# Interleaving the columns of two weight blocks in a float32 decoder layer, so that the matmuls read with a step of two

## The chip, the cores and the metric

The kernel runs on one core of one Trainium2 chip. The metric is the device time of one execution in microseconds (us), less being better. The core's engines are TensorE (PE: matmuls; PEld: the loads of its stationary operand), VectorE (DVE), ScalarE (ACT), GpSimd (POOL) and SyncE (SP), which here issues most of the DMAs. All matmul operands lie in SBUF, the on-chip memory of 128 partitions; matmuls accumulate into PSUM banks of 128 x 512 float32.

## The reference

One decoder layer on 256 tokens of width 2048, in float32. An input projection feeds two token mixers (16-head latent attention and a short causal convolution), each gated with SiLU. What concerns the change is the end, in which five matrices of 2048 x 2048 are applied to 256 tokens:

```python
g_mla, g_conv = h @ w_in[..., -4096:-2048], h @ w_in[..., -2048:]
y_mla  = einsum('bse,ed->bsd', attn, w_o_mla)
y_conv = einsum('bse,ed->bsd', b_gate * conv * silu(z_conv), w_o_conv)
merged = sigmoid(g_mla) * y_mla + sigmoid(g_conv) * y_conv
out    = einsum('bsd,de->bse', merged, w_out)
x      = x + _rmsnorm(out, post_norm_g)
```

(The first line is shortened: the two gates are the last 4,096 columns of the projection of the normalised input `h`.)

## The kernel before

*Precision.* Every float32 matrix product is made of three matmuls on rounded parts (type float32r): a value is split into `hi` (rounded by ACT, L245) and `lo` (the rest, by DVE, L246), and `product` issues `hi*hi`, `hi*lo` and `lo*hi` into the same PSUM bank (L88 is the line of all matmuls). The stationary operand is a block of 128 x 128 of the activations (128 features, 128 tokens), the moving operand a block of 128 x 512 of the weights: 128 input features in the partitions, 512 output columns in a row. One matmul gives 128 tokens by 512 output columns.

*Weights.* All weights come through one list of units, `plan`, in the order of use. A unit is 128 x 2048 float32 (1,024 KB), that is four blocks of 128 x 512, for four neighbouring groups of 128 input features (k4 = 0 to 3) of one quarter of the output columns. `load_raw` brings a unit into one of three `raw` buffers (L161, SP's queue), `split_unit` splits each half of it (`HALF` = 1,024 columns, so two blocks) into a tile `whi` and a tile `wlo` of 128 x 1024, and `take` returns `piece(j, n)`, which cuts the j-th block of n columns out of the half in which it lies: block 0 and 1 out of the first pair of tiles, 2 and 3 out of the second.

*Merged stage* (matmuls named `sq`). Over four quarters c of the output columns, over the four matrices n (two gates from `x_both`, the attention's output product from `at_both`, the convolution's from `cv_both`), over four units kk, over two token tiles t and the four blocks k4 of the unit: a `product` each. That is 4 x 4 x 4 x 2 x 4 x 3 = 1,536 matmuls. Its units are `u_d[c][n][kk]`.

*Output product* (matmuls named `out`). Over four column quarters and four units, two token tiles and four blocks, from `m_both`: 4 x 4 x 2 x 4 x 3 = 384 matmuls; its units are `u_out[c, kk]`, which come last in the plan. Each stage's units come out of the array `wsq` (five matrices), which the host lays out before the launch; the device time has no part of that. In the ending the second token tile's result is finished with three small plain-float32 matmul pairs (`fin`).

*Order.* Matmuls stand in the order in which they are written; a scheduler places the rest around them, and SP's loads wait until a `raw` buffer is free. Stages ahead of the merged one read units of other arrays (`cv` and `z` matmuls among them, which have the same shape of 128 x 512).

Of the kernel before, what the change touches and what calls it, by code (L numbers as in the profile page):

```python
# [18 lines left out]
P = 128  # L19
# [18 lines left out]
UNIT = 2048  # L38
LINE = 32
HALF = UNIT // 2  # L40
# [42 lines left out]
def tile_layer(ctx: ExitStack, tc: tile.TileContext, xw, w0, xb, x, pos, pvec, post_g, wc, wz, wcv, wkr, wqk, wqr, wv, cwr, wsq, out):  # L83
# [22 lines left out]
    def add(ap, width=UNIT):  # L106
        plan.append((ap, width))
        return len(plan) - 1
# [30 lines left out]
    u_d = [[[add(wsq[n, c, k]) for k in range(4)] for n in range(4)] for c in range(4)]  # L139
# [62 lines left out]
    def ahead(i, raw=3, split=1):  # L202
        while done["raw"] < min(i + raw, len(plan)):
            load_raw(done["raw"])
            done["raw"] += 1
        while done["split"] < min(i + 1 + split, len(plan)):
            while done["raw"] <= done["split"]:
                load_raw(done["raw"])
                done["raw"] += 1
            split_unit(done["split"])  # L210
            done["split"] += 1

    def take(i):
        ahead(i)
        parts = splits.pop(i)

        def piece(j, n):
            o = j * n
            h, o = o // HALF, o % HALF
            return parts[h][0][:, o : o + n], parts[h][1][:, o : o + n]  # L220

        return piece
# [81 lines left out]
    n = 2 * XW // S  # L304
# [202 lines left out]
    for i in range(KD // 2):  # L507
# [3 lines left out]
        w = take(u_qa[i])  # L511
# [3 lines left out]
    for i in range(4):  # L515
        w = take(u_ckv[i])
# [9 lines left out]
    w = splits.pop(u_kr)  # L526
# [150 lines left out]
    def values(h, pt):  # L677
        vv = groups["v", h // HV]
        j = h % HV
        o = bank(f"o{h}", tag="o", bufs=1)  # L680
        vs = slice(j * DV, (j + 1) * DV)
        both = o[:, :].rearrange("p (i q) -> p i q", i=2)
        mm = matmul
        mm(both, vv[0][:, 0, vs], pt[:, :, :S], start=True, stop=False)
        yield
        mm(o[:, :S], vv[1][:, 0, vs], pt[:, 0, :S], start=False, stop=False)
        mm(o[:, P:S], vv[1][:, 1, vs], pt[:, 0, S:], start=False, stop=False)
        mm(both[:, :, P:], vv[0][:, 1, vs], pt[:, :, S:], start=False, stop=True)

        at = at_t[:, h // HV, :, :].rearrange("p t (i k x) -> p t i k x", i=4, k=HV)[:, :, :, j, :]  # L690
        f = temp("f")
        whole(f[:, :], o)
        nc.vector.tensor_tensor(at, f[:, :].rearrange("p (t i x) -> p t i x", t=NT, i=4), at, op=ALU.mult)
# [119 lines left out]
    for h in range(H):  # L813
        v, at = divmod(h, HV)

        if at == 0:
            for i in range(4):
# [13 lines left out]
                elif v and i == 2:  # L831
                    o = values(h - 1, pt)
# [171 lines left out]
    for i, (c, kk) in enumerate(out_order[:3]):  # L1004
        w = take(u_out[c, kk])
# [188 lines left out]
```

## Time and profile before

| What | Value |
|---|---|
| Median of 2 runs | 1035.01 us (1034.82 and 1035.21) |
| Span of the profiled execution, first to last instruction | 1033.7 us |
| Merged stage (`sq`), from 590.5 to 938.7 us | 348.2 us, 1,536 matmuls |
| Output product (`out`), from 938.7 to 1025.7 us | 87.0 us, 384 matmuls |
| Ending after the last `out` matmul | 8 us |
| Mean granted TensorE clock | 1.000 |
| HBM traffic | 221 GB/s over the span |

The profile is of one execution. The only time of its own that it has is its span; the two timed runs lie 1.1 and 1.5 us above it. A matmul's duration in it (389 ns for 512 columns) is longer than the distance from one matmul's start to the next, since they overlap in the array; the pace is read from the starts, or from a piece's length over its count. `out<-in` names the tile that an instruction writes and those that it reads. An arrow behind an idle time names what ended it.

### The profile page before, as it was taken

What the parts mean: (1) busy time and instruction counts of PE and PEld (TensorE: products, weight loads), DVE (VectorE), ACT (ScalarE), POOL (GpSimd) and SP (SyncE); (2) the same over time, 40 slices, a digit from 0 to 9 for tenths busy, and PEclk for the clock granted to TensorE, in tenths of its full rate; (3) what the DMA queues carried; (4) which work ended last, traced back from release to release, by engine and by line L of the source; (5) the groups of instructions that cost most, each with busy time, mean ns of one, the idle gap of its engine ahead of it and who ended that gap; (6) DMA issues with size and microseconds to landing.
All of it is one profiled execution on the core that took longest, in us unless ns stands there. A gap on an engine that the chain in (4) does not pass through costs nothing.

```text
span 1033.7 us, 12740 instructions
## 1 busy us (share of the span) xinstructions
PE 1027.6 (99%) x4684; PEld 856.7 (83%) x4684; DVE 683.5 (66%) x957; ACT 527.4 (51%) x735; POOL 178.7 (17%) x344
## 2 busy tenths in 40 slices
PE   9999999999999999999999999999999999999998
PEld 8888888888888888888888888888888888888886
DVE  7588787787777777777777785564455455455562
ACT  7665545655456454564555565344434444443451
POOL 4540421104300223112133120020010001002000
PEclk9999999999999999999999999999999999999999
DMA  9775865668665676857686765565565557558642
GB/s 353 278 261 204 276 221 219 211 197 288 215 250 193 223 265 209 275 187 242 228 270 226 265 217 199 204 226 185 200 219 209 188 201 241 183 188 337 228 163 81
DMA packets 44526, 233.25 MB, mean 226 GB/s; under 512 B 7952, under 2 KB 10512, under 8 KB 21552
## 3 DMA queue, kind: packets, MB, share of 16 engines
q1 hardware_dynamic: 32400, 199.67, 54.6%
q0 software_dynamic: 11632, 29.48, 8.8%
q10 hardware_dynamic: 432, 3.29, 0.8%
q8 instruction: 36, 0.59, 0.2%
q14 instruction: 26, 0.21, 0.1%
HBM read 215.66 MB, written 12.58 MB: 221 GB/s over the span
## 4 chain that ended last, share of the span: by engine, by line
PE 96%; DMA 2%; ACT 1%; DVE 0%; issue 0%; DVEq 0%; SPq 0%
PE cv L88 34%; PE sq L88 34%; PE out L88 8%; PE z L88 6%; PE qa L88 2%; PE vv L88 2%; PE kn L88 2%; PE qn L88 2%; PE ckv L88 2%; PE sc L88 1%; PE qr L88 1%; PE o L88 1%; DMA raw<-wz_dram 1%; DMA at_f<-far_qa 1%; DMA at_f<-far_ckv 0%
## 5 line engine op out<-in xcount | busy, mean ns | idle before, releaser
L246 DVE TENSOR_TENSOR wlo<-raw,whi 128x1024 fp32r<-128x1024 f32 (+1 forms) x370 | 440.5, 1196 | 279.8 <-ACT whi L245 268.4
L245 ACT ACTIVATE whi<-raw 128x1024 fp32r<-128x1024 f32 (+1 forms) x372 | 382.4, 1035 | 401.6 <-PE sq L88 180.5
L88 PE MATMUL cv<-whi,x_both 128*128 128x512 f32 x1024 | 319.8, 389 | 0.0
L88 PEld LDWEIGHTS cv<-whi,x_both 128*128 128x128 f32 x1024 | 192.3, 188 | 39.4
L88 PE MATMUL cv<-wlo,x_both 128*128 128x512 f32 x512 | 199.6, 390 | 0.0
L88 PE MATMUL sq<-whi,x_both 128*128 128x512 f32 x512 | 158.3, 389 | 0.0
L88 PEld LDWEIGHTS sq<-whi,x_both 128*128 128x128 f32 x512 | 96.1, 188 | 19.9
L88 PEld LDWEIGHTS cv<-wlo,x_both 128*128 128x128 f32 x512 | 96.1, 188 | 19.5 <-DVE wlo L246 0.2
L88 PE MATMUL sq<-wlo,x_both 128*128 128x512 f32 x256 | 99.6, 389 | 0.0
L88 PE MATMUL z<-whi,x_both 128*128 128x512 f32 x256 | 80.0, 389 | 0.0
L88 PE MATMUL sq<-whi,at_both 128*128 128x512 f32 x256 | 79.5, 389 | 0.0
L88 PE MATMUL sq<-whi,cv_both 128*128 128x512 f32 x256 | 79.5, 389 | 0.0
L88 PE MATMUL out<-whi,m_both 128*128 128x512 f32 x256 | 78.9, 389 | 0.0
L328 POOL DMA_DIRECT2D far<-sg x32 | 17.5, 553 | 313.0 <-DVE sg L320 238.4
L328 POOL DMA_DIRECT2D far<-via x64 | 35.1, 556 | 177.9 <-DVE via L320 177.9
L88 PEld LDWEIGHTS sq<-wlo,x_both 128*128 128x128 f32 x256 | 48.0, 188 | 10.0
L88 PEld LDWEIGHTS sq<-whi,at_both 128*128 128x128 f32 x256 | 48.0, 188 | 9.9
L88 PEld LDWEIGHTS out<-whi,m_both 128*128 128x128 f32 x256 | 48.0, 188 | 9.9
L88 PEld LDWEIGHTS sq<-whi,cv_both 128*128 128x128 f32 x256 | 48.0, 188 | 9.9
L88 PEld LDWEIGHTS z<-whi,x_both 128*128 128x128 f32 x256 | 48.1, 188 | 9.9
L88 PE MATMUL z<-wlo,x_both 128*128 128x512 f32 x128 | 49.8, 389 | 0.0
L88 PE MATMUL sq<-wlo,at_both 128*128 128x512 f32 x128 | 49.8, 389 | 0.0
(216 smaller groups left out, 1128.9 us busy)
## 6 DMA issues: line engine op xcount, KB each, us to landing
raw<-wsq_dram SPq DMA_DIRECT2D x80, 1024.0 KB, 4.8
raw<-wcv_dram SPq DMA_DIRECT2D x64, 1024.0 KB, 5.6
raw<-wz_dram SPq DMA_DIRECT2D x16, 1024.0 KB, 4.9
raw<-wqk_dram SPq DMA_DIRECT2D x8, 1024.0 KB, 6.0
cw<-cwr_dram POOLq DMA_DIRECT2D x24, 256.0 KB, 6.0
raw<-wc_dram SPq DMA_DIRECT2D x4, 1024.0 KB, 10.5
raw<-wv_dram SPq DMA_DIRECT2D x4, 1024.0 KB, 4.8
far<-via POOLq DMA_DIRECT2D x64, 48.0 KB, 4.1
```

The costliest lines, as they stand in the source:

```text
L88: return tc.keep_in_program_order(nc.tensor.matmul(*a, **kw))
L245: a = nc.scalar.activation(hi, src, AF.Copy)
L246: b = nc.vector.tensor_tensor(lo, src, hi.bitcast(F32), op=ALU.subtract)
L328: tc.keep_in_program_order(queue.dma_start(out=f[i], in_=m))
```

## The change

In `wsq` the host now lays the two blocks of each half unit out alternately: element 2i of a half is column i of its first block, element 2i + 1 is column i of its second. The device moves and splits the halves as before. `piece`, for the units of the merged stage and the output product (all units from `u_d[0][0][0]` on), returns a view that begins at element 0 or 1 of the half and takes every second one: 512 elements with a step of 8 bytes. What each matmul computes, and the order of all instructions on every engine, stay the same; the other stages' units and views are unchanged.

```diff
         def piece(j, n):
             o = j * n
             h, o = o // HALF, o % HALF
+            if i >= u_d[0][0][0]:
+                hi, lo = (a[:, :].rearrange("p (c k) -> p k c", k=HALF // n)[:, o // n] for a in parts[h])
+                return hi, lo
             return parts[h][0][:, o : o + n], parts[h][1][:, o : o + n]
...
         "wsq": np.stack([
-            w.reshape(4, 4, P, 4, 512).transpose(3, 0, 2, 1, 4).reshape(4, 4, P, UNIT)
+            w.reshape(4, 2, 2, P, 4, 512).transpose(4, 0, 3, 1, 5, 2).reshape(4, 4, P, UNIT)
             for w in (g_m, g_c, w_o_mla, w_o_conv, w_out)
         ]),
```

## The prediction, made before the changed kernel ran

> **What bounds the kernel now.** I read the page first, then the chain that ended last, then the stages the change touches, in the view by stretches, and at the end single matmuls in the timeline.
>
> The page's first part gives busy time, share of the span and instruction count of each engine; the clock row of its second part gives the granted TensorE clock in 40 slices; the last row quoted is the share of the engines in the chain of waits.
>
> ```profile
> span 1033.7 us, 12740 instructions
> PE 1027.6 (99%) x4684; PEld 856.7 (83%) x4684; DVE 683.5 (66%) x957; ACT 527.4 (51%) x735; POOL 178.7 (17%) x344
> PEclk9999999999999999999999999999999999999999
> PE 96%; DMA 2%; ACT 1%; DVE 0%; issue 0%; DVEq 0%; SPq 0%
> ```
>
> TensorE (PE) is busy all the time at the full granted clock and carries 96% of the chain. A busy PE need not run at its peak, so its waits have to be seen too: this is the view of waits, for PE alone, over the whole run (waited in all, times, longest).
>
> ```profile
> PE idle L88 <- PEq L1182: 0.8, 1, 0.8
> PE fin L88 <- ACT dg L1069: 0.4, 1, 0.4
> PE vv L88 <- DVE f L396: 0.2, 1, 0.2
> ```
>
> Neither a load, nor ScalarE (ACT), nor VectorE (DVE) holds PE back by as much as 2 us. What is left as a price is the pace of the matmul stream itself. The chain in order of time (start, length, what) shows the two pieces that read the rearranged weights, and they are its last long ones; the stretches below it are the merged stage and the output product (length, busy time and records of PE, PEld, DVE, ACT, POOL, then clock, DMA share, GB/s).
>
> ```profile
> 590.51 348.20 PE sq L88 x1536
> 938.71 87.05 PE out L88 x384
> ```
>
> ```profile
> 590.50:938.70 348.20, 348.20 (x1538) 288.29 (x1537) 192.77 (x190) 156.43 (x168) 22.22 (x41) 1.00 0.59 206
> 938.70:1025.70 87.00, 87.00 (x386) 72.03 (x385) 45.46 (x49) 36.04 (x46) 5.28 (x10) 1.00 0.55 205
> ```
>
> So from 590.5 to 1025.7 us the time is 1,920 matmuls back to back: 348.20 / 1536 = 226.7 ns each, and 87.05 / 384 = 226.7 ns each. DVE is busy 55% of the first stretch and ACT 45%, DMA 59%: each has room. After 1025.7 some 8 us of ending follow, which the change doesn't touch.
>
> **The change part by part.** It alters two things: the order in which the host lays out `wsq`, and the address pattern with which the matmuls of those units read the moving operand.
>
> *Instructions, waits and order.* On all five engines the instructions stand in the same order with the same waits as before; nothing is added, removed or moved. Cost nothing, and no cover is used up.
>
> *Loads and splits.* A unit is still one transfer of 1,024 KB, contiguous in each partition, and ACT and DVE still go over it in pieces of 1,024 neighbouring elements. In the merged stage, grouped by form:
>
> ```profile
> L246 DVE TENSOR_TENSOR wlo<-raw,whi 128x1024 fp32r<-128x1024 f32 x129 | 157.9, 1224 | 152.4 <-ACT whi L245 147.2
> L245 ACT ACTIVATE whi<-raw 128x1024 fp32r<-128x1024 f32 x128 | 135.6, 1060 | 180.2 <-PE sq L88 180.2
> ```
>
> The values in them change place, their number and addresses don't: nothing, and if I am wrong there the idle time beside them (152.4 and 180.2 us) takes it.
>
> *The stationary operand.* `x_both`, `at_both`, `cv_both` and `m_both` are read as before, 128 neighbouring columns per load: nothing.
>
> *The moving operand.* This is the one real edit. Each of the 1,920 matmuls read 512 neighbouring 4-byte elements per partition (2,048 bytes); now it reads every second one of 1,024 (a span of 4,096 bytes). They all lie on the path that sets the end, with nothing to hide them, so whatever one of them costs more is paid 1,920 times. No row of the trace has a moving operand with a step between elements: by the kernel's text every one is made of runs of 128 neighbours or more. So the price is to be bounded.
>
> First, what in the 226.7 ns depends on the number of columns. In the timeline (start, length, what) eight matmuls of 512 columns stand ahead of eight of 256, and the next kind starts at once behind them:
>
> ```profile
> 133.77 1.12 PE L88 MATMUL kn<-ckv,wlo 128*128 128x256 f32 x8
> 134.73 0.40 PE L88 MATMUL cv<-whi,x_both 128*128 128x512 f32 x1
> ```
>
> (134.73 - 133.77) / 8 = 120 ns for 256 columns. Against 226.7 ns for 512 that makes 106.7 ns per 256 columns, that is 0.417 ns a column, and a fixed part of 120 - 106.7 = 13.3 ns, about the same in either size. While its columns stream, a matmul takes 4 bytes per 0.417 ns, 9.6 bytes per ns in each partition. ACT and DVE, the other readers, take 1,024 elements in 1,060 and 1,224 ns, about 3.9 and 3.3 bytes per ns from each operand. So this stream is already read 2.5 times as fast as any other, and if the memory fetches by neighbouring bytes, the strided one would need 19.2.
>
> The two ends, with the value I take:
> - Lower end, below nothing: the step costs nothing and by luck removes the fixed 13.3 ns as well: 1,920 x 13.3 ns = 25.5 us off. I give that little, since that part shows in 256 and 512 columns alike and so isn't tied to how a column is fetched.
> - Nothing: the array takes a column each 0.417 ns and the fetch can supply every second element at that rate.
> - Upper end: a strided read costs what reading its whole span costs, two slots of 226.7 ns: 1,920 x 226.7 = 435.3 us more.
> - Taken: the 512 columns stream at half rate, the fixed part is paid once: 512 x 0.417 = 213.3 ns more per matmul, 440.0 in place of 226.7. 1,920 x 213.3 ns = 409.6 us.
>
> I take this end and not nothing, because the row nearest to a strided read of 1,024 places is a contiguous one of that span, and no row shows any reader receiving more than these 9.6 bytes per ns in one stream. It is a choice: the trace shows that much being delivered, not that more could not be.
>
> **The sum.** The profiled span is 1033.7 us; the median of the two runs is 1035.0, 1.3 us more for what lies around the span. Untouched: 590.5 us ahead and 8 us behind. Merged stage: 348.2 + 1,536 x 0.2133 = 675.8 us. Output product: 87.05 + 384 x 0.2133 = 169.0 us. 1033.7 + 327.6 + 81.9 = 1443.2 us of span, so **1444.6 us**. PE becomes later everywhere, so nothing else can become the bound: loads, splits and evictions have twice the time.
>
> **The rivals.**
>
> *No change (not slower): the fetch has room for a step of two.* One wide access to the memory would bring several neighbouring elements, contiguous reading would use them all, and with every second one used there are still enough for one column per 0.417 ns. It decides as long as a fetch is at least twice as wide, or fast, as the contiguous stream needs. For it: the matmul's rate may be the array's and not the memory's. Two rows of the ending hint at that, one from the timeline and one from the list of a tile's instructions (durations in ns, least/median/most):
>
> ```profile
> 1025.59 1.46 PE L88 MATMUL fin<-xr,ident 128*128 128x256 f32 x6
> ```
>
> ```profile
> L88 PE MATMUL fin<-xr,ident x6: 377/378/379, 1025.6 to 1026.7; 128*128 128x256 f32 x6
> ```
>
> These are three plain-float32 matmuls of 256 columns in two records each, (1460 - 378) / 5 = 216 ns a record instead of 120; the operand is read contiguously, and still the array takes it slower, so there the fetch isn't what limits. Against it: it says nothing of the faster stream. Time: 1035 us, give or take the few us of a repeat.
>
> [...] No row of this trace shows a strided read that could confirm it, and I leave it weaker than doubling for that reason.
>
> *Part of the doubling.* The memory delivers more than one stream uses. The 256-column matmuls above get 256 moving and 128 stationary elements, 1,536 bytes, each 120 ns: 12.8 bytes per ns. If that were one shared supply, counted by span, a strided matmul would need (4,096 + 512) / 12.8 = 360 ns, 133 more than now: 1,920 x 0.133 = 256 us, **1291 us**. For it: the row. Against it: it needs both reads to share a supply, and nothing shows them to.
>
> [...]
>
> *Worse than doubling.* The step throws the matmul to a rate like plain float32's, two records of some 216 ns for 256 columns: 864 ns for 512, 1,920 x 0.637 = 1,224 us more, 2259 us. Nothing speaks for it but that such a rate exists.
>
> *Faster.* The lower end above: 1035.0 - 25.5 = 1009.5 us.
>
> **How the numbers follow.** Doubling 0.53, part of it 0.15, worse 0.02: slower by over 2% together 0.70. No change 0.27. Faster by over 2% 0.03. (2% is about what a measurement of this kernel can tell from no change.) The predicted time is that of doubling, 1444.6; its own range is 1417 (the fixed part hidden behind the longer stream: 25.5 us + 2 less) to 1472 (two whole slots, 1470.3, and 1.5 for repeats). No change alone has more than the 2 in 10 that may be left out, so the whole range reaches down to it: 1031 to 1472; left out are faster and worse.
>
> **What would show it.** Right: in the changed kernel's chain the `sq` piece is near 676 us and the `out` piece near 169, matmuls of these two start 440 ns apart in the timeline, while `cv` and `z` stay at 227; PE still waits for nothing and the clock stays 1.00; ACT's idle time behind `sq` grows by over 300 us. No change: both pieces stay within 1% of 348 and 87. The shared supply: starts 360 ns apart. A PE wait of several us for DVE, ACT or a load in these stages would refute the claim that splits and loads are untouched, and a slower `cv` the claim that only the moving operand counts. The forecast is wrong if matmuls with a step keep 0.417 ns a column.

## The result, and the profile after

The changed kernel takes 1470.55 us (median of two runs, 1470.13 and 1470.96) against 1035.01 before. The ratio is 1.4207, with a 95% interval from 1.4173 to 1.4242: slower by 435.5 us. Its profiled execution took 1470.96 us, with a span of 1468.9.

The page of the changed kernel: busy time of each engine, the clock, and the engines' shares of the chain that ended last.

```profile
span 1468.9 us, 12740 instructions
PE 1462.7 (100%) x4684; PEld 894.8 (61%) x4684; DVE 686.0 (47%) x957; ACT 529.3 (36%) x735; POOL 180.2 (12%) x344
PEclk9999999999999999999999999999999999999999
PE 99%; DMA 0%; ACT 0%; DVE 0%; issue 0%
```

The instruction counts are those of before, and the busy times of DVE, ACT and POOL within 1%. PE has grown by 435.1 us, at the same full clock. The weight loads (PEld) have grown by 38.1 us: the profile gives a load of these two stages 207 to 208 ns in place of 188, though they read the same contiguous operand; they lie beside the matmuls. The chain in order of time (start, length, what) ends with these pieces:

```profile
584.46 5.48 PE cv L88 x24
590.51 696.34 PE sq L88 x1536
1286.85 174.09 PE out L88 x384
```

Both pieces that read the interleaved blocks have doubled, 348.20 to 696.34 and 87.05 to 174.09. That is 453.3 to 453.4 ns a matmul, in place of 226.7. The merged stage begins at 590.51 us as before, to the hundredth, and the `cv` piece ahead of it keeps its pace; this is its line in the kernel before:

```profile
584.45 5.48 PE cv L88 x24
```

After the last `out` matmul 8.0 us follow, as before. So the whole loss, 348.14 + 87.04 = 435.2 us, lies in these 1,920 matmuls.

The stretches of the two stages (length, then busy time and records of PE, PEld, DVE, ACT, POOL, clock, DMA share, GB/s) and PE's waits (total, times, longest) show that nothing else became late:

```profile
590.50:1286.90 696.40, 696.40 (x1538) 318.76 (x1537) 196.05 (x191) 157.46 (x169) 24.26 (x44) 1.00 0.30 103
1286.90:1461.00 174.10, 174.10 (x386) 79.70 (x385) 45.08 (x48) 36.22 (x47) 3.31 (x6) 1.00 0.28 101
```

```profile
PE idle L88 <- PEq L1185: 0.8, 1, 0.8
PE fin L88 <- ACT dg L1072: 0.4, 1, 0.4
PE qa L88 <- ACT whi L248: 0.3, 1, 0.3
```

Same records, same DVE and ACT work, half the DMA rate (103 and 101 GB/s against 206 and 205), no wait of PE over 0.8 us. The page's row of ACT's splits (after the second bar the idle time ahead of them and what ended most of it) shows who waits now:

```profile
L248 ACT ACTIVATE whi<-raw 128x1024 fp32r<-128x1024 f32 (+1 forms) x372 | 382.3, 1034 | 762.6 <-PE sq L88 495.9
```

ACT idles 495.9 us behind `sq` matmuls, some 180 before: it waits for PE.

### The profile page after: what moved, and what is told of

Read it like the earlier page. It is cut to its first block, busy times and chain, and to the rows that moved or that the text cites. A ratio compares the mean times of both kernels' runs of the same rounds, so it can differ in the third digit from the quotient of the medians.

```text
span 1468.9 us, 12740 instructions
## 1 busy us (share of the span) xinstructions
PE 1462.7 (100%) x4684; PEld 894.8 (61%) x4684; DVE 686.0 (47%) x957; ACT 529.3 (36%) x735; POOL 180.2 (12%) x344
## 4 chain that ended last, share of the span: by engine, by line
PE 99%; DMA 0%; ACT 0%; DVE 0%; issue 0%
PE sq L88 47%; PE cv L88 24%; PE out L88 12%; PE z L88 6%; PE qa L88 2%; PE kn L88 2%; PE qn L88 2%; PE vv L88 1%; PE ckv L88 1%; PE sc L88 1%; PE qr L88 1%; PE o L88 1%; PE kr L88 0%; DMA raw<-w_dram 0%; PE fin L88 0%; ACT junk L1025 0%
## 5 line engine op out<-in xcount | busy, mean ns | idle before, releaser
L248 ACT ACTIVATE whi<-raw 128x1024 fp32r<-128x1024 f32 (+1 forms) x372 | 382.3, 1034 | 762.6 <-PE sq L88 495.9
L88 PE MATMUL sq<-whi,x_both 128*128 128x512 f32 x512 | 278.5, 632 | 0.0
L88 PEld LDWEIGHTS sq<-whi,x_both 128*128 128x128 f32 x512 | 106.2, 207 | 125.6 <-issue 125.6
L88 PE MATMUL sq<-wlo,x_both 128*128 128x512 f32 x256 | 161.7, 632 | 0.0
L88 PE MATMUL sq<-whi,cv_both 128*128 128x512 f32 x256 | 139.6, 632 | 0.0
L88 PE MATMUL sq<-whi,at_both 128*128 128x512 f32 x256 | 139.6, 632 | 0.0
L88 PE MATMUL out<-whi,m_both 128*128 128x512 f32 x256 | 139.1, 632 | 0.0
L88 PEld LDWEIGHTS out<-whi,m_both 128*128 128x128 f32 x256 | 53.1, 208 | 62.9 <-issue 62.2
L88 PE MATMUL sq<-wlo,at_both 128*128 128x512 f32 x128 | 80.9, 632 | 0.0
L88 PE MATMUL sq<-wlo,cv_both 128*128 128x512 f32 x128 | 80.9, 632 | 0.0
L88 PE MATMUL out<-wlo,m_both 128*128 128x512 f32 x128 | 80.9, 632 | 0.0
```

Source lines behind the costliest of these rows:

```text
L88: return tc.keep_in_program_order(nc.tensor.matmul(*a, **kw))
L248: a = nc.scalar.activation(hi, src, AF.Copy)
```

## The experiments

Each kernel was run once, beside the kernel before on the same chip (1035.46 to 1035.78 us). "A matmul" below means the length of the `sq` piece over its 1,536 matmuls. What each pattern does with groups of four neighbouring float32 (16 bytes, counted from a tile's start, called lines below) turned out to be the key, as e5, e10 and e11 show (232.2, 453.3 and 226.7 ns), so the table has it:

| Run | Moving operand of the 512 columns | Used of a line at one visit | ns a matmul | us in all |
|---|---|---|---|---|
| before | contiguous | 4 | 226.7 | 1035.0 |
| after | every second element | 2 | 453.3 | 1470.6 |
| e1_pairs | pairs, aligned to 8 bytes | 2 | 453.3 | 1471.0 |
| e2_crossed | elements 1, 2 or 0, 3 of four | 2 | 453.3 | 1470.4 |
| e3_step4 | every fourth element, two sequences | 1 | 461.3 | 1486.0 |
| e5_fours | runs of 4 on line borders | 4 | 232.2 | 1047.9 |
| e6_sixteens | runs of 16 on line borders | 4 | 240.0 | 1061.0 |
| e8_shifted | contiguous, begun 8 bytes off | 4, the ends 2 | 232.2 | 1045.8 |
| e10_fours_off | runs of 4 over line borders | 2 | 453.3 | 1470.5 |
| e11_in_line | whole lines, order 0, 2, 1, 3 | 4 | 226.7 | 1035.5 |

**e1_pairs.** Against the changed kernel; the host lays out pairs to match, and the PSUM operand is written as the same 512 columns.

```diff
-                hi, lo = (a[:, :].rearrange("p (c k) -> p k c", k=HALF // n)[:, o // n] for a in parts[h])
+                hi, lo = (a[:, :].rearrange("p (c k r) -> p k c r", k=HALF // n, r=2)[:, o // n] for a in parts[h])
```

> The two blocks of a half alternate in pairs of neighbouring columns (8 bytes read, 8 bytes left out) in place of single columns. Three theories of why a strided matmul takes 453.4 ns in place of 226.7. Eight-byte words: the moving operand is fetched as aligned words of two float32, one word in the time of two columns, and a word of which one half is used costs as much as a full one; then pairs cost nothing, 226.7 ns a matmul and about 1035 us in all. Sixteen-byte lines: the fetch brings four float32 in the time of four columns and half of each is left unused here too; then 453.4 ns and about 1470 us. Half-rate mode: any pattern whose innermost step isn't 1 streams at half rate, however much of a word it uses; the innermost step here is 1, so about 1035 us.

Its chain:

```profile
590.09 696.33 PE sq L88 x1536
1286.43 174.09 PE out L88 x384
```

1471.01 us: both pieces as with single columns. Eight-byte words fall, since here every such word is used whole, and a matmul still takes 453.3 ns. The half-rate mode, as it was worded (innermost step other than 1), falls too.

**e2_crossed.** Against the changed kernel; the host's order and the shape of the PSUM operand match.

```diff
-                hi, lo = (a[:, :].rearrange("p (c k) -> p k c", k=HALF // n)[:, o // n] for a in parts[h])
+                v = [a[:, :].rearrange("p (c r) -> p c r", r=4) for a in parts[h]]
+                hi, lo = (a[:, :, 0::3] if o else a[:, :, 1:3] for a in v)
```

> Of every four neighbouring elements one block takes the second and third (a pair that crosses the border of an aligned 8-byte word, inside one 16-byte line), the other block the first and fourth (a step of three, then one). Eight-byte words: each column needs a word of its own in both blocks, all 1,920 matmuls at 453.4 ns, about 1470 us. Sixteen-byte lines: two used of four in both blocks, also about 1470 us. Half-rate mode: the first block is a run of two with innermost step 1 and keeps 226.7 ns, the second has innermost step 3 and takes 453.4, so starts alternate between the two by block, and the time is about 1253 us.

The `sq` piece of its chain:

```profile
590.22 696.34 PE sq L88 x1536
```

1470.38 us, and the timeline has no alternation by block: the whole piece is as long as with single columns. Which two elements of a line are used doesn't matter; this is as lines of 16 bytes would have it.

**e3_step4.** Against the changed kernel; the host's order and the shape of the PSUM operand match.

```diff
-                hi, lo = (a[:, :].rearrange("p (c k) -> p k c", k=HALF // n)[:, o // n] for a in parts[h])
+                hi, lo = (a[:, :].rearrange("p (c q) -> p q c", q=4)[:, 2 * o // n : 2 * o // n + 2] for a in parts[h])
```

> A step of four elements (16 bytes): the half unit holds four interleaved sequences of 256 columns, a matmul reads two of them one after the other, 512 columns as before. Eight-byte words: one used element per word as with a step of two, so the same 453.4 ns and about 1470 us. Sixteen-byte lines: one used element of four, twice as bad, about 907 ns a matmul: 1,920 x 680 ns = 1306 us more, about 2341 us. Half-rate mode: any step the same, about 1470 us.

Its chain:

```profile
590.34 708.60 PE sq L88 x1536
1298.94 177.16 PE out L88 x384
```

1485.96 us, 461.3 ns a matmul. The lines' forecast of 907 ns is refuted: a line of which one element is used costs hardly more per column than one of which two are. So a fixed time per line doesn't stand; what is left is a slow rate of about 0.89 ns a column, against 0.443 (226.7 / 512), and the question of what a pattern must have to escape it.

**e4_stationary.** Against the kernel before, the stationary operand alone with a step of two:

```diff
-                    a = [cols[:, k, o + t * P : o + (t + 1) * P] for o in (0, S)]
+                    a = [cols[:, k, o : o + S].rearrange("p (c t) -> p t c", t=NT)[:, t] for o in (0, S)]
```

(and the same for `m_both` in the output product).

> The kernel before with its contiguous weights, but in the merged stage and the output product the stationary operand is read with a step of two (even tokens for one tile, odd tokens for the other); tokens then stand in another order from there on and meet other tokens' scales, the amount of work is the same. If a load of the stationary operand also streams at half rate, its 128 columns take some 107 ns longer (256 columns contiguous stream in 106.7 ns). A load now takes 188 ns and begins as the matmul before it begins. If the next matmul has to wait for the whole load, the pace becomes 188 + 107 + 39 = 334 ns and the time 1035 + 1,920 x 0.107 = 1240 us; if loads are pipelined deeper (120 ns pace of the 256-column matmuls), the longer load still fits beside 213 ns of streaming, and the time stays within 25 us of 1035. If only the moving operand knows the price: 1035 us exactly.

Its chain, and the group of the loads in the `sq` stage (count, busy us, mean ns, idle before):

```profile
589.72 358.38 PE sq L88 x1536
948.10 89.61 PE out L88 x384
```

```profile
L88 PEld LDWEIGHTS sq<-whi,x_both 128*128 128x128 f32 x512 | 98.8, 193 | 20.6
```

1047.73 us. A load takes 193 ns in place of 188, a matmul 233.3 in place of 226.7. This is within the 25 us that a longer load still beside the streaming was given, so a step of two in the stationary operand alone is far from doubling the time here; in the changed kernel, where the time doubled, that operand has no step. It doesn't show that a stepped load is nearly free. Contiguous loads seem to follow each other every 115 to 120 ns where they set the pace (a reading of e9 and of the trace of the kernel before, below). If the step doubled that, a load would take an estimated 230 to 240 ns, nearly all of it beside the 226.7 ns of a matmul, and set a pace like the 233.3 measured. No run tests this; beside shorter matmuls the price could be larger.

**e5_fours and e6_sixteens.** The view of e1 with `r=4` and `r=16`, the host's layout to match.

```diff
-                hi, lo = (a[:, :].rearrange("p (c k) -> p k c", k=HALF // n)[:, o // n] for a in parts[h])
+                hi, lo = (a[:, :].rearrange("p (c k r) -> p k c r", k=HALF // n, r=4)[:, o // n] for a in parts[h])
```

> The two blocks alternate in runs of four neighbouring columns (16 bytes read, 16 left out, on 16-byte borders). Pairs cost as much as single columns, crossed pairs the same and a step of four hardly more, so what is left: Whole lines: the full rate needs all four elements of a 16-byte line, and whatever uses less of a line goes column by column at half rate; then 226.7 ns a matmul and about 1035 us. Long runs: the full rate needs a run longer than four (128 neighbours have it in the kernel before); then 453.4 ns and about 1470 us. A price per break between runs: single columns and pairs, with 511 and 255 breaks, cost the same, so it would have to be capped; if each break costs a fixed 0.9 ns or more (226.7 ns over 255), 127 breaks cost 113 ns or more: 1035 + 1,920 x 0.113 = 1252 us.

> The same in runs of 16 columns (64 bytes read, 64 left out). Whole lines: free, about 1035 us. Long runs: 1035 us if 16 neighbours are long enough, 1470 us if not; this halves the stretch in which the length must lie. A price per break of 0.9 ns: 31 breaks, 28 ns a matmul, 1035 + 54 = 1089 us.

The `sq` piece of the fours, then of the sixteens:

```profile
592.29 356.70 PE sq L88 x1536
```

```profile
589.96 368.64 PE sq L88 x1536
```

1047.90 and 1060.99 us. Four neighbours on a line's border bring the full rate back, all but 5.5 ns a matmul (232.2 less 226.7). A price per break is refuted by order: 127 breaks cost less than 31. So is a price by span: these matmuls reach over the same 4,096 bytes as those of the changed kernel. Why sixteens lose 13.3 ns, more than fours, no run here explains.

**e7_half_step2.** Against the changed kernel, both stages call this in place of `product`:

```diff
+    def by_halves(ps, a, b, k):
+        if k in (0, KD - 1):
+            return product(ps[:, :], a, b, k == 0, k == KD - 1)
+        for m in (slice(0, S), slice(S, 2 * S)):
+            product(ps[:, m], a, [v[:, m] for v in b], False, False)
```

> The changed kernel with its step of two, but each matmul of 512 columns in two of 256, except for the first and the last feature block of each sum: 3,360 matmuls of 256 columns and 240 of 512. It tells whether the fixed 13.3 ns of a matmul doubles with the step, the 25.9 us by which the forecast fell short (453.4 in place of 440.0 ns). If every part of a matmul's slot doubles: 2 x 120 = 240 ns each, 3,360 x 240 + 240 x 453.4 = 915.2 us for both stages, 44.8 more than the 870.4 of the changed kernel, about 1515 us. If the columns take 0.886 ns each (453.4 / 512) and nothing is fixed: 226.7 ns each, about 1470 us. If columns take 0.833 ns and 26.7 ns are fixed: again 240 ns and about 1515 us.

Its chain:

```profile
590.69 695.92 PE sq L88 x2880
1286.61 173.99 PE out L88 x720
```

1470.34 us, no more than with matmuls of 512. (695.92 + 173.99 - 240 x 0.4534) / 3,360 = 226.5 ns for 256 columns: 0.885 ns a column in either size. With a step of two no fixed part of a matmul shows.

**e8_shifted.** Against the kernel before, for the units of the two stages:

```diff
+            if i >= u_d[0][0][0]:
+                o = o - 2 if o else 2
             return parts[h][0][:, o : o + n], parts[h][1][:, o : o + n]
```

> The kernel before, contiguous, but in the two stages each block is read from two elements (8 bytes) beside its start: elements 2 to 513 and 510 to 1021 of a half. Two columns of each block are thereby those of its neighbour. Whole lines: if only whole lines on 16-byte borders count, the first and last line of each matmul are half used, four columns of 512 at half rate, 1.7 ns a matmul, at most 1038 us; if four neighbours must lie within one line for the rate to hold at all, every group straddles a border: 453.4 ns and about 1470 us. Long runs: no price, 1035 us.

Its chain:

```profile
590.19 356.70 PE sq L88 x1536
946.89 89.19 PE out L88 x384
```

1045.81 us, 232.2 ns a matmul: no half rate, but 5.5 ns where at most 1.7 were expected. So the groups of four needn't begin with the matmul. The bound of 1.7 ns was too tight; where the other 3.8 ns arise, at the two half-used ends or elsewhere, the run doesn't show.

**e9_half_contig.** The same `by_halves` in the kernel before.

```diff
-                    product(pss[t][:, :], a, w(k4, 512), k == 0, k == KD - 1)
+                    by_halves(pss[t], a, w(k4, 512), k)
```

> The kernel before, contiguous, with the same cut into matmuls of 256 columns as in the run of half matmuls with a step of two (3,360 of 256 columns and 240 of 512). The forecast took from eight matmuls of another stage that 256 columns take 120 ns, so that 13.3 ns of a matmul were fixed. If so: 3,360 x 120 + 240 x 226.7 = 457.6 us for both stages, 22.3 more than the 435.3 of the kernel before, about 1057 us. If nothing is fixed and a column takes 226.7 / 512 = 0.443 ns: 113.4 ns each, 435.4 us, about 1035 us. If the loads of the stationary operand, now twice as many, can't follow at that pace, more than 1057 us.

Its chain, and the stretch of the merged stage with PEld as the second busy time:

```profile
591.24 366.61 PE sq L88 x2880
957.85 91.67 PE out L88 x720
```

```profile
591.20:957.80 366.60, 366.60 (x2882) 358.32 (x2881) 192.82 (x190) 155.99 (x168) 22.30 (x41) 1.00 0.58 196
```

1059.25 us: (366.61 + 91.67 - 240 x 0.2267) / 3,360 = 120.2 ns for 256 contiguous columns, as the forecast had read it. But PEld is now busy 358.32 of 366.60 us, 98%, where before it was 83%. So the 120 ns may be the pace of the loads and not 106.7 ns of streaming with 13.3 fixed. This run doesn't tell the two apart, but the trace of the kernel before says more: it has a single matmul of 128 columns between two of 256 (timeline: start, length, what).

```profile
554.94 0.28 PE L88 MATMUL sc<-kn,qn_hi 128*128 128x256 f32 x1
555.05 0.22 PE L88 MATMUL sc<-kn,qn_lo 128*128 128x128 f32 x1
555.11 0.34 PE L88 MATMUL sc<-kr,qr 128*128 128x256 f32 x1
555.28 0.40 PE L88 MATMUL sc<-kn,qn_hi 128*128 128x256 f32 x2
```

From start to start the first 256 columns take 0.11 us, the 128 columns 0.06, and the second 256 columns 0.17. The trace has 32 such places, 26 of them behind a matmul of 512 columns as here, with 113 or 114, 60 and 170 or 171 ns. The forecast's 13.3 ns and 0.417 ns a column would give 120, 67 and 120. At 0.443 ns a column and nothing fixed, 256 columns take 113 ns, which the first matmul shows behind one of 512; and the 170 ns are more than columns can explain, as the same number takes 113 and 120 elsewhere. The matmul of 128 and the one behind it together take 230 ns, two times 115. Each matmul has one load (4,684 of each on the page), and no two loads of that trace start less than 108 ns apart, so this speaks for the loads, at one per 115 to 120 ns, as what set the 120 ns. It is a reading of the trace; no run changed the loads alone.

**e10_fours_off.** Against the changed kernel, with the layout of before:

```diff
-                hi, lo = (a[:, :].rearrange("p (c k) -> p k c", k=HALF // n)[:, o // n] for a in parts[h])
+                hi, lo = (a[:, :].rearrange("p (c r) -> p c r", r=8)[:, :, 2:6] for a in parts[h])
```

> Runs of four neighbours as in the run of aligned fours, which kept nearly the full rate (232 ns a matmul), but begun two elements later, so that each run takes the second half of one 16-byte line and the first half of the next: elements 2 to 5 of every eight. Both blocks of a half read the same columns here, so one block's columns stand in for the other's. Whole lines: every line is half used, as with pairs: 453.4 ns, about 1470 us. Run length: four neighbours are enough wherever they begin (a contiguous block begun two elements off its border took 232 ns): about 1048 us.

The `sq` piece of its chain:

```profile
590.37 696.34 PE sq L88 x1536
```

1470.54 us: the same runs of four as in e5, moved by 8 bytes, and the half rate is back. Run length falls, whole lines stand.

**e11_in_line.** Against the changed kernel; the host orders each group of four so that the columns come out in their old order.

```diff
-                hi, lo = (a[:, :].rearrange("p (c k) -> p k c", k=HALF // n)[:, o // n] for a in parts[h])
+                hi, lo = (a[:, o : o + n].rearrange("p (c x y) -> p c y x", x=2, y=2) for a in parts[h])
```

> Contiguous blocks, every 16-byte line wholly used by one matmul, but its four elements are taken in the order first, third, second, fourth (the host lays them so that the result is the same). Whole lines: four hits in each line one after the other, so about 1035 to 1050 us. Run length: no two columns that follow each other are neighbours, so they go one by one: 453.4 ns, about 1470 us.

Its chain:

```profile
590.46 348.20 PE sq L88 x1536
938.66 87.05 PE out L88 x384
```

1035.45 us, both pieces to the hundredth those of the kernel before. This matmul steps by two elements at every second column, and forward and back, in a pattern of three dimensions within the partition; it costs nothing, as it should if what counts is that each line is used up before the next.

**e12_split_undoes.** Against the changed kernel: `wsq` stays interleaved, the contiguous view of `piece` is back, and the split undoes the interleaving.

```diff
+            if i >= u_d[0][0][0]:
+                src = t[:, h : h + n].rearrange("p (c k) -> p k c", k=2)
+                split_act(*(a[:, :].rearrange("p (k c) -> p k c", k=2) for a in (hi, lo)), src)
+                parts.append((hi, lo))
+                continue
```

> The interleaved layout in memory stays, but ACT and DVE undo it while they split: they read every second element of the raw unit and write contiguous blocks, so the matmuls read contiguously again. Matmuls at 226.7 ns. If a step of two costs ACT and DVE nothing, about 1035 us. If it doubles their 1,060 and 1,224 ns for 1,024 elements: in the merged stage DVE gets 193 + 158 = 351 us to do in 348, ACT 156 + 136 = 292, so DVE is just at the edge and waits of PE appear: 1040 to 1070 us.

Its chain, and the two groups of splits in the merged stage (count, busy us, mean ns, idle before and what ended it):

```profile
589.49 348.20 PE sq L88 x1536
937.69 87.05 PE out L88 x384
```

```profile
L251 DVE TENSOR_TENSOR wlo<-raw,whi 128x1024 fp32r<-128x1024 f32 x129 | 157.9, 1224 | 153.0 <-ACT whi L250 152.7
L250 ACT ACTIVATE whi<-raw 128x1024 fp32r<-128x1024 f32 x128 | 145.7, 1138 | 171.5 <-PE sq L88 171.5
```

1034.64 us, the time of the kernel before (1035.49 beside it). The matmuls are at 226.7 ns again. With a step of two DVE takes the same 1,224 ns, ACT 1,138 in place of 1,060, and ACT's 78 ns disappear in its idle time.

## Why the prediction held, and where its size was off

*The bound and the untouched parts.* Right. PE's stream was the price, each matmul's extra was paid 1,920 times, and order, loads, splits, the first 590.5 us and the ending of 8 us didn't move. PE nowhere waits longer than 0.8 us, as before.

*The size.* 1444.6 us were forecast, 1470.55 measured, 25.9 us more. The term that was mis-sized is the fixed part of 13.3 ns, in the step "the fixed part is paid once". The two stages took 870.4 us, which is 1,920 x 453.3 ns, the end that the forecast called two whole slots (1470.3 us). Half matmuls show why: with the step 256 columns take 226.5 ns and 512 take 453.3, so nothing is fixed and a column takes 0.885 ns, not 0.833 with 13.3 ns beside it. The 13.3 ns came from eight contiguous matmuls of 256 columns at 120 ns against 226.7 for 512. Two lengths always yield a time per column and a fixed part; they can't show that there is one, and "about the same in either size" was assumed, not found. The same cut in the two stages repeats the 120 ns with the loads busy 98% of the time, and where the loads had time ahead, behind a matmul of 512, the trace has 113 or 114 ns. So the 120 ns was most likely the pace of the loads and not of the columns. Whether a small fixed part is left in the contiguous stream stays open.

*The reason.* The forecast argued that a strided read costs what its span costs. That was wrong although the number came out near: runs of four and of sixteen reach over the same 4,096 bytes at 232 and 240 ns, and with a step of four, where a matmul's two sequences together reach over 8,192 bytes, four slots of 226.7 would be 907 ns, but 461.3 were measured. That a step of two costs just what its span would is luck. (The supporting count, "2.5 times as fast as any other", was a little high: ACT reads 2,048 elements in 1,901 ns at L361, 4.3 bytes per ns, which makes it 2.2. Nothing hangs on it.) What the runs show is a fast and a slow rate. Where all four elements of each 16-byte line are taken before the next line, a column takes 0.44 to 0.47 ns, also in the order first, third, second, fourth, and also where a contiguous block begins off a line's border. Where two or one of a line are taken at a visit, it takes 0.885 to 0.90 ns. Three of a line were not tried.

*No change.* Refuted for a step of two. Its core, that one wide access serves several columns, fits the runs if the access is the line and all four of its elements must be used; they show the pace, not the access itself. In this float32r stream two elements of a line at a visit run at half rate in four different patterns (every second, pairs, crossed, off fours: 453.3 ns a matmul), all four at the full one, 226.7 ns, or near it (232.2 and 240.0).

*Part of the doubling* (a shared supply, 360 ns a matmul, 1291 us): refuted, the starts are 453 ns apart. A step in the stationary operand costs 6.6 ns a matmul of 512 columns, and a step in both operands was not tried. *Worse* and *faster* didn't come.

## What to carry to other kernels

As these runs show it, a matmul's moving operand in float32r should use up each 16-byte line (four elements) before it goes to the next; the one other order within the line that was tried cost nothing (226.7 ns a matmul), gaps between whole lines 2 and 6 per cent of a matmul (232.2 and 240.0 ns), but lines used by half at a visit halved the rate of a stream that bounds the kernel (453.3 ns). If a layout must interleave, let it alternate in runs of whole lines on 16-byte borders (four and sixteen columns were tried), or undo it in an elementwise pass that has idle time beside it, as the splits here. A price per matmul read off matmuls of another size has to be looked at for what sets their pace: here 256 columns took 120 ns where the loads were busy 98% of the time, and 113 or 114 ns behind a matmul of 512.

## What the runs showed of the hardware that wasn't expected

One element used of each line costs hardly more than two: 461.3 against 453.3 ns for 512 columns. So the slow rate is a time per column, about 0.885 ns (twice 0.443), and not one per line; how the four-element case escapes it, these runs don't show.

Small prices without an explanation: 5.5 ns a matmul for a contiguous block begun 8 bytes off (and the same for runs of four), 13.3 ns for runs of sixteen, 6.6 ns for a stationary operand with a step of two beside 512 columns (a possible reason stands at e4).

DVE reads every second element of one operand at the contiguous pace (1,224 ns for 1,024), ACT at 1,138 in place of 1,060 ns: the step that halves TensorE's stream costs nothing on the one and 7% on the other of these two engines, which take 1.0 to 1.2 ns an element.
